# Squares summed by one-column matmuls at the start of a diffusion backbone, and the final features transposed to tokens on partitions before the last norm

## The chip, the cores and the metric

One core of one Trainium2 chip runs the whole program. The time is device microseconds of one execution; runs are compared by their median. A run counts as faster or slower in the chances below when it differs by over 0.2%.

## What is computed

A backbone of two layers over 256 latent and 256 context tokens of width 1024. Each layer is a half-step SwiGLU FFN, a token mixer and another half-step FFN; every sub-layer is preceded by an RMS norm whose gain and shift are modulated by a product of the condition with w_mod. A final RMS norm gives the latent tokens.

```python
def _rmsnorm(h, g):
    y = h32 * lax.rsqrt(jnp.mean(h32 * h32, axis=-1, keepdims=True) + NORM_EPS)
    return (y * g.astype(jnp.float32)).astype(h.dtype)
...
def _ffn_half(h, g, shift, scale, gate, w_in, w_out):
    a, b = jnp.split(_modnorm(h, g, shift, scale) @ w_in, 2, axis=-1)
    return h + 0.5 * gate * ((jax.nn.silu(a) * b) @ w_out)
...
    return _rmsnorm(h, final_norm_g)
```

## The kernel before

The features lie on the partitions: 1024 is eight k-tiles of 128, and a token is a column. hl holds the latent tokens, hc the context tokens. All weights are fp32 in memory and are split into a rounded part hi (ACT, line 124) and a rest lo (DVE, line 125); a product is three matmuls (mm3, lines 136 to 138): the weights' hi by the tokens' hi, hi by the tokens' rest, lo by the tokens' hi. unit() makes such a pair of 2048 columns in two halves, from two loads of 512 KB into seven raw buffers on SP's queue.

The program begins with keep_warm: 22 products of the identity with itself (line 106), while the tokens arrive in eight loads. first() is the start of the first FFN. square() squares two k-tiles at a time on ACT (line 231) and adds them up on DVE (lines 237, 239); rstd_cols() sums over the partitions with one-column matmuls (line 255), and rsqrt() takes the root on DVE with Newton steps (lines 208 to 221). mod_slice(k) gives gain and shift of one k-tile: two loads of wm0, eight matmuls in four column groups (line 155), a copy by ACT (mr, line 160), two matmuls with sel (line 163) and two additions on DVE (line 164). After slice 0 eight more keep-warm products run on its buffer. The root is broadcast over the partitions by four matmuls with the identity (line 271), copied to memory by DVE (line 417), and modnorm() makes ut (DVE, line 285), u's hi (ACT, line 288) and u's rest (DVE, line 289) of each half of the tokens.

lead() then multiplies the first three units of w_in k-tile by k-tile as these become ready: for each of eight k-tiles three units by two halves by three matmuls of 512 columns, 144 in all. swiglu() takes the result: sil (ACT line 305, DVE line 306) and its split g (lines 132, 133). The fourth unit and those after it follow one by one. Beside this DVE computes further modulation pieces (line 176). The instruction order of each engine is fixed when the program is built, by a scheduler that works from the dependences and its own estimates; add_manual_dep adds orders that it must keep.

At the end finish() scales the eight k-tiles by the final gain (ACT, line 831), rstd(0) sums the squares, takes the root and broadcasts it, DVE multiplies four tiles (line 834) and SP sends each off (line 835), with features still on partitions.

Of the kernel before, what the change touches and what calls it, by code (L numbers as in the profile page):

```python
# [11 lines left out]
F32 = mybir.dt.float32  # L12
F32R = mybir.dt.float32r
I32 = mybir.dt.int32
AF = mybir.ActivationFunctionType
# [18 lines left out]
def hybrid_kernel(ctx: ExitStack, tc: tile.TileContext, small, conds, xT, wm0, wm, w_in, w_out,  # L34
# [72 lines left out]

    keep_warm(ident, 22)

# [6 lines left out]

    def unit(src, n=2048, behind=None, at=0):

        hi = hip.tile([P, 2048 + 64], F32R, tag="hi", name=nm("hi"))[:, at:at + 2048]
        lo = lop.tile([P, 2048 + 64], F32R, tag="lo", name=nm("lo"))[:, at:at + 2048]  # L120
        for a in range(0, n, 1024):
            b = min(n, a + 1024)
            raw = load(src[:, a:b])
            A.activation(hi[:, a:b], raw, AF.Copy)  # L124
            i = V.tensor_tensor(lo[:, a:b], raw, hi[:, a:b].bitcast(F32), op=ALU.subtract).ins  # L125
            if behind is not None:
                tc.add_manual_dep(i, behind.name, mybir.DependencyInfo(
                    mybir.DependencyClass.NoSync, mybir.DependencyReason.DATA), reason="order")
        return hi, lo
# [18 lines left out]
    def mod_slice(j):  # L148
# [3 lines left out]
        for kk in range(2):  # L152
            for g in range(4):
                kt = 2 * g + kk
                T.matmul(ps[32 * g:32 * g + 32, :256], c32[:, kt, :], raw[kt // 4][:, kt % 4 * 256:(kt % 4 + 1) * 256],  # L155
                         start=(kk == 0), stop=(kk == 1), tile_position=(0, 32 * g))
        if j == 0:
            keep_warm(raw[1], 8)
        rows = wk.tile([P, 256], F32, tag="ut", name=nm("mr"), bufs=4)
        A.activation(rows, ps[:, :256], AF.Copy)  # L160
        pc = stat()
        for c in range(2):
            T.matmul(pc[:, 2 * c:2 * c + 2], rows[:, c * P:(c + 1) * P], sel, start=True, stop=True)
            V.tensor_tensor(mods[0, c][:, :, j], pc[:, 2 * c:2 * c + 2], bias[:, 0, c, j:j + 1].to_broadcast([P, 2]),
                            op=ALU.add)

    def mod_piece(l, c, n, kp):
# [57 lines left out]

    def square(k, v, n=1):
        sq = wk.tile([P, NT], F32, tag="sil", name=nm("sq"), bufs=3)
        if n == 1:
            A.activation(sq[:, :NL], H(k, v), AF.Square)
        else:  # L230
            A.activation(sq.rearrange("p (k n) -> p k n", k=2),
                         hl[k // 2] if v == 0 else hc[k // 4][:, k % 4:k % 4 + 2, :], AF.Square)
        for i in range(n):
            s = sq[:, i * NL:(i + 1) * NL]
            if k + i == 0:
                sq_sum[v] = wk.tile([P, NL], F32, tag=f"ss{v}", name=nm("ss"), bufs=1)
                V.tensor_copy(sq_sum[v], s)
            else:
                V.tensor_tensor(sq_sum[v], sq_sum[v], s, op=ALU.add)  # L239

# [7 lines left out]
    def rstd_cols(*vs):  # L248
        ps = stat()
        n = 2 * len(vs)  # L250
        for i in range(n):
            v, o = vs[i // 2], i % 2 * P
            parts = [sq_sum[v]] + [sq_last[w] for w in (v,) if w in sq_last]
            for j, t in enumerate(parts):
                T.matmul(ps[:, i:i + 1], t[:, o:o + P], mean_col, start=j == 0, stop=j == len(parts) - 1)  # L255
        ms = wk.tile([P, 4], F32, tag="ms", name=nm("ms"))[:, :n]
        V.tensor_scalar(ms, ps[:, 0:n], EPS, None, op0=ALU.add)
# [3 lines left out]

    def rstd(*vs, meanwhile=None):
        n = 2 * len(vs)
        y = rstd_cols(*vs)
        if meanwhile is not None:
            meanwhile()
        for v in vs:
            normed[v] = newest[0]
        pr = stat()
# [40 lines left out]

    def in_unit(l, i, f, behind=None, at=0):
        return [x.rearrange("p (k s c) -> p k s c", k=KT, s=2) for x in unit(w_in[l, i, f], behind=behind, at=at)]

# [94 lines left out]
    def first(g, u):  # L408
        for c in range(2):
            mod_tile(0, c)  # L410
        gain = cst.tile([P, 2, KT], F32, name="gain0_0")
        units = []
        for v in range(2):
            for k in range(0, KT, 2):
                square(k, v, 2)
        pb = gtile(F32)
        V.tensor_copy(pb, rstd(0, 1, meanwhile=lambda: mod_slice(0)))
        pr = [pb[:, a:b] for a, b in HALVES]

# [18 lines left out]
        for k in range(2):  # L438
            ready(k)
            units.append(in_unit(0, 0, k, normed[0]))  # L440
        units.append(in_unit(0, 0, 2))
# [386 lines left out]
    def finish(v):  # L828
        ts = [gtile(F32).rearrange("p (k n) -> p k n", k=2) for _ in range(4)]
        for k in range(KT):  # L830
            A.activation(ts[k // 2][:, k % 2, :], H(k, 0), AF.Copy, scale=sm[:, S_FG + k:S_FG + k + 1])
        pr = rstd(0)[:, :NL].rearrange("p (k n) -> p k n", k=1).to_broadcast([P, 2, NL])
        for j in range(4):
            V.tensor_tensor(ts[j], ts[j], pr, op=ALU.mult)
            nc.sync.dma_start(out[:, 2 * j:2 * j + 2, :], ts[j])

# [45 lines left out]
def build(arrays):  # L882
# [3 lines left out]
    args = [nc.dram_tensor(f"in_{n}", a.shape, F32, kind="ExternalInput").ap() for n, a in arrays]  # L886
    args.append(nc.dram_tensor("out_x", (P, KT, NL), F32, kind="ExternalOutput").ap())
    with tile.TileContext(nc) as tc:
# [12 lines left out]
```

## Time and profile before

| what | us |
|---|---|
| median of 3 runs | 1679.08 |
| lowest and highest | 1678.54, 1679.54 |
| the profiled execution's own time | 1678.37 |
| its span, first to last instruction | 1676.6 |

The profile is of one execution, 0.71 us below the median; 1.77 us lie around its span. Its views are read as follows: the chain of waits goes back from the last instruction to what released each step; a timeline gives an engine's instructions with the idle time before them and what ended it; windows give busy time and the clock that TensorE was granted (1.00 is 2.4 GHz, 0.50 is 1.2 GHz). Matmul ends are modelled, so starts are the safer numbers.

### The profile page before, as it was taken

Reading aid. Unit: us, or ns where it says so; the run is one execution under the profiler, and the core shown is the slowest. Engines: PE = TensorE matmul, PEld = TensorE weight load, DVE = VectorE, ACT = ScalarE, POOL = GpSimd, SP = SyncE. Lnnn points to the kernel's source line nnn. Section 1 sums busy time; section 2 is a strip of 40 time slices with the busy share of each in tenths; the row PEclk is TensorE's granted clock in tenths of the full one; section 3 lists DMA queues with packets and bytes.
Section 4 is the critical chain, followed back from the end, with each engine's and each line's share of the span. In section 5 each row is a group of like instructions: output and inputs, shape, how many; then the busy total and the mean of one; then the engine's idle time right before and its main releaser. Section 6 shows DMA issues by size and latency. Waiting matters only on the chain.

```text
span 1676.6 us, 23555 instructions
## 1 busy us (share of the span) xinstructions
PE 1655.2 (99%) x9368; PEld 1441.9 (86%) x9368; DVE 1114.6 (66%) x2015; ACT 599.7 (36%) x918; POOL 1.3 (0%) x7
## 2 busy tenths in 40 slices
PE   8999999999999999999999999999999999999997
PEld 6788888889998888888898888888988998899997
DVE  5886677578567845855776546544796767685554
ACT  4431222235433222212342223222574444464443
POOL 0000000000000000000000000000000000000000
PEclk9999999999999999999999999999999999999998
DMA  9675555442215634644435544544334333345651
GB/s 326 238 229 178 176 176 192 141 146 91 67 61 184 202 133 140 200 147 138 139 102 173 178 151 151 189 140 149 108 119 139 121 131 126 133 150 202 194 167 50
DMA packets 73263, 258.74 MB, mean 154 GB/s; under 512 B 8129, under 2 KB 8513, under 8 KB 73153
## 3 DMA queue, kind: packets, MB, share of 16 engines
q1 hardware_dynamic: 73152, 257.24, 45.6%
q8 instruction: 73, 1.20, 0.3%
q14 instruction: 38, 0.30, 0.1%
HBM read 256.16 MB, written 1.05 MB: 153 GB/s over the span
## 4 chain that ended last, share of the span: by engine, by line
PE 95%; DVE 3%; ACT 1%; issue 1%; DMA 0%; SPq 0%; DVEq 0%; ACTq 0%
PE mm L137 31%; PE mm L138 31%; PE mm L136 31%; PE st L155 1%; DVE lo L125 1%; PE st L255 1%; ACT hi L124 0%; DMA big<-in_xT 0%; DVE g L133 0%; PE st L271 0%; DVE g L498 0%; DVE u L289 0%; PE st L106 0%; PE st L731 0%; DVE ss L239 0%
## 5 line engine op out<-in xcount | busy, mean ns | idle before, releaser
L124 ACT ACTIVATE hi<-raw 128x1024 fp32r<-128x1024 f32 x346 | 345.4, 1031 | 653.5 <-PE mm L137 460.6
L137 PE MATMUL mm<-u,hi 128*128 128x512 f32 (+1 forms) x1568 | 554.3, 354 | 0.0
L136 PE MATMUL mm<-u,hi 128*128 128x512 f32 (+1 forms) x1568 | 553.0, 354 | 1.2 <-ACT u L288 1.2
L138 PE MATMUL mm<-u,lo 128*128 128x512 f32 (+1 forms) x1568 | 553.6, 354 | 0.0
L125 DVE TENSOR_TENSOR lo<-raw,hi 128x1024 fp32r<-128x1024 f32 x346 | 406.2, 1195 | 56.8 <-ACT hi L124 52.5
L137 PE MATMUL mm<-g,hi 128*128 128x256 f32 (+1 forms) x1000 | 332.8, 333 | 0.8 <-DVE g L133 0.4
L136 PE MATMUL mm<-g,hi 128*128 128x256 f32 (+1 forms) x1000 | 332.6, 334 | 0.7 <-ACT g L132 0.7
L138 PE MATMUL mm<-g,lo 128*128 128x256 f32 (+1 forms) x1000 | 332.4, 333 | 0.0
L136 PEld LDWEIGHTS mm<-u,hi 128*128 128x128 f32 x1568 | 293.9, 188 | 44.5 <-ACT u L288 2.3
L137 PEld LDWEIGHTS mm<-u,hi 128*128 128x128 f32 x1568 | 294.3, 188 | 42.1 <-DVE u L289 1.0
L138 PEld LDWEIGHTS mm<-u,lo 128*128 128x128 f32 x1568 | 293.9, 188 | 41.8 <-issue 1.2
L176 DVE CUSTOM_DVE_ANT_0 prod<-raw,big,sm 128x1024 bf16<-128x1024 f32 x224 | 275.7, 1282 | 0.0
L306 DVE TENSOR_TENSOR sil<-sil,mm 128x512 f32<-128x512 f32 (+1 forms) x90 | 54.3, 604 | 240.6 <-PE mm L138 231.3
L137 PEld LDWEIGHTS mm<-g,hi 128*128 128x128 f32 x1000 | 187.8, 188 | 20.7 <-DVE g L133 1.6
L136 PEld LDWEIGHTS mm<-g,hi 128*128 128x128 f32 x1000 | 187.4, 188 | 20.2 <-ACT g L132 1.0
L138 PEld LDWEIGHTS mm<-g,lo 128*128 128x128 f32 x1000 | 187.8, 188 | 19.0
L368 DVE SCALAR_TENSOR_TENSOR hl<-mm,gate,hl 128x256 f32<-128x256 f32 x96 | 46.4, 483 | 145.2 <-PE mm L138 145.0
L305 ACT ACTIVATE sil<-mm 128x512 f32<-128x512 f32 (+1 forms) x90 | 47.6, 530 | 204.7 <-PE mm L138 204.7
L133 DVE TENSOR_TENSOR g<-sil,g 128x512 fp32r<-128x512 f32 (+1 forms) x92 | 55.2, 600 | 3.2 <-ACT g L132 3.2
L132 ACT ACTIVATE g<-sil 128x512 fp32r<-128x512 f32 (+1 forms) x92 | 50.3, 547 | 9.0 <-DVE sil L306 9.0
L288 ACT ACTIVATE u<-ut,mod 128x256 fp32r<-128x256 f32 x72 | 33.1, 499 | 42.0 <-DVE ut L285 42.0
L138 PE MATMUL mm<-hi,g 128*128 128x256 f32 (+1 forms) x128 | 43.0, 336 | 0.5 <-DVE g L498 0.4
(174 smaller groups left out, 1208.3 us busy)
## 6 DMA issues: line engine op xcount, KB each, us to landing
raw<-in_w_in SPq DMA_DIRECT2D x176, 512.0 KB, 4.5
raw<-in_wm SPq DMA_DIRECT2D x144, 512.0 KB, 4.8
raw<-in_w_out SPq DMA_DIRECT2D x80, 512.0 KB, 4.3
raw<-in_wvg SPq DMA_DIRECT2D x32, 512.0 KB, 4.3
raw<-in_wqk SPq DMA_DIRECT2D x16, 512.0 KB, 4.6
raw<-in_wro SPq DMA_DIRECT2D x16, 512.0 KB, 4.3
raw<-in_w_out SPq DMA_DIRECT2D x16, 256.0 KB, 2.7
raw<-in_wf SPq DMA_DIRECT2D x8, 512.0 KB, 3.8
```

What stands on the lines that cost most here:

```text
L124: A.activation(hi[:, a:b], raw, AF.Copy)
L125: i = V.tensor_tensor(lo[:, a:b], raw, hi[:, a:b].bitcast(F32), op=ALU.subtract).ins
L132: A.activation(hi, src, AF.Copy)
L133: V.tensor_tensor(lo, src, hi.bitcast(F32), op=ALU.subtract)
L136: T.matmul(ps, l[0], r[0], start=first, stop=False)
L137: T.matmul(ps, l[0], r[1], start=False, stop=False)
L138: T.matmul(ps, l[1], r[0], start=False, stop=last)
L176: V.tensor_tensor_reduce(t, raw, crow[v], 1.0, bias[:, l, c, k:k + 1], ALU.mult, ALU.add, mods[l, c][:, v, k:k + 1])
L288: A.activation(u[k][0][:, a:b], t, AF.Identity, bias=s)
L305: i = A.activation(s[:, :n], pab[0][:, :n], AF.Silu).ins
L306: j = V.tensor_tensor(s[:, :n], s[:, :n], pab[1][:, :n], op=ALU.mult).ins
L368: V.scalar_tensor_tensor(H(d, v), ps[:, x - a:y - a], gate[:, v, d:d + 1], H(d, v), op0=ALU.mult, op1=ALU.add)
```

## The change

The keep-warm products at the start use a tile that DVE fills (14 instead of 22). Each pair of squared k-tiles goes straight to PE: four one-column matmuls (line 426 of the new file) add it to four columns of one PSUM bank, in 32 matmuls; DVE adds nothing. Slice 0 runs after the sums, then the root; three keep-warm products on the last squares replace the eight on slice 0's buffer. The first ut reads the broadcast root in PSUM, and the copy to memory comes later. ACT's copy of slice 0 is ordered ahead of the second halves of the first two units' rounding. At the end every scaled k-tile is transposed by PE (line 862), three quarters of them ahead of the sums; the root then is a number per partition, so that the broadcast falls away, and DVE (line 872) and ACT (line 874) multiply two blocks each, which leave in four transfers, three by SP and one by ACT's queue. The output's layout is tokens by features.

```diff
--- before.py
+++ after.py
@@ -105,7 +105,9 @@
         for _ in range(n):
             T.matmul(ps[:, :P], x[:, :P], x[:, :P], start=True, stop=True)
 
-    keep_warm(ident, 22)
+    warm = gtile(F32)[:, :P]
+    V.memset(warm, 1.0)
+    keep_warm(warm, 14)
 
 
     def load(src):
@@ -114,18 +116,23 @@
         nc.sync.dma_start(t[:, :n], src)
         return t[:, :n]
 
-    def unit(src, n=2048, behind=None, at=0):
+    def order(i, behind):
+        tc.add_manual_dep(i, behind.name, mybir.DependencyInfo(
+            mybir.DependencyClass.NoSync, mybir.DependencyReason.DATA), reason="order")
+
+    def unit(src, n=2048, behind=None, at=0, ahead=None):
 
         hi = hip.tile([P, 2048 + 64], F32R, tag="hi", name=nm("hi"))[:, at:at + 2048]
         lo = lop.tile([P, 2048 + 64], F32R, tag="lo", name=nm("lo"))[:, at:at + 2048]
         for a in range(0, n, 1024):
             b = min(n, a + 1024)
             raw = load(src[:, a:b])
-            A.activation(hi[:, a:b], raw, AF.Copy)
+            i = A.activation(hi[:, a:b], raw, AF.Copy).ins
+            if ahead is not None and a:
+                order(i, ahead)
             i = V.tensor_tensor(lo[:, a:b], raw, hi[:, a:b].bitcast(F32), op=ALU.subtract).ins
             if behind is not None:
-                tc.add_manual_dep(i, behind.name, mybir.DependencyInfo(
-                    mybir.DependencyClass.NoSync, mybir.DependencyReason.DATA), reason="order")
+                order(i, behind)
         return hi, lo
 
     def split(hi, lo, src):
@@ -154,15 +161,14 @@
                 kt = 2 * g + kk
                 T.matmul(ps[32 * g:32 * g + 32, :256], c32[:, kt, :], raw[kt // 4][:, kt % 4 * 256:(kt % 4 + 1) * 256],
                          start=(kk == 0), stop=(kk == 1), tile_position=(0, 32 * g))
-        if j == 0:
-            keep_warm(raw[1], 8)
         rows = wk.tile([P, 256], F32, tag="ut", name=nm("mr"), bufs=4)
-        A.activation(rows, ps[:, :256], AF.Copy)
+        i = A.activation(rows, ps[:, :256], AF.Copy).ins
         pc = stat()
         for c in range(2):
             T.matmul(pc[:, 2 * c:2 * c + 2], rows[:, c * P:(c + 1) * P], sel, start=True, stop=True)
             V.tensor_tensor(mods[0, c][:, :, j], pc[:, 2 * c:2 * c + 2], bias[:, 0, c, j:j + 1].to_broadcast([P, 2]),
                             op=ALU.add)
+        return i
 
     def mod_piece(l, c, n, kp):
 
@@ -223,20 +229,14 @@
 
     sq_sum = {}
 
-    def square(k, v, n=1):
-        sq = wk.tile([P, NT], F32, tag="sil", name=nm("sq"), bufs=3)
-        if n == 1:
-            A.activation(sq[:, :NL], H(k, v), AF.Square)
+    def square(k, v):
+        sq = wk.tile([P, NT], F32, tag="sil", name=nm("sq"), bufs=3)[:, :NL]
+        A.activation(sq, H(k, v), AF.Square)
+        if k == 0:
+            sq_sum[v] = wk.tile([P, NL], F32, tag=f"ss{v}", name=nm("ss"), bufs=1)
+            V.tensor_copy(sq_sum[v], sq)
         else:
-            A.activation(sq.rearrange("p (k n) -> p k n", k=2),
-                         hl[k // 2] if v == 0 else hc[k // 4][:, k % 4:k % 4 + 2, :], AF.Square)
-        for i in range(n):
-            s = sq[:, i * NL:(i + 1) * NL]
-            if k + i == 0:
-                sq_sum[v] = wk.tile([P, NL], F32, tag=f"ss{v}", name=nm("ss"), bufs=1)
-                V.tensor_copy(sq_sum[v], s)
-            else:
-                V.tensor_tensor(sq_sum[v], sq_sum[v], s, op=ALU.add)
+            V.tensor_tensor(sq_sum[v], sq_sum[v], sq, op=ALU.add)
 
     sq_last = {}
 
@@ -253,19 +253,21 @@
             parts = [sq_sum[v]] + [sq_last[w] for w in (v,) if w in sq_last]
             for j, t in enumerate(parts):
                 T.matmul(ps[:, i:i + 1], t[:, o:o + P], mean_col, start=j == 0, stop=j == len(parts) - 1)
+        return root(ps, n)
+
+    def root(ps, n):
         ms = wk.tile([P, 4], F32, tag="ms", name=nm("ms"))[:, :n]
         V.tensor_scalar(ms, ps[:, 0:n], EPS, None, op0=ALU.add)
         y = wk.tile([P, 4], F32, tag="rs", name=nm("rs"))[:, :n]
         rsqrt(y, ms, n)
         return y
 
-    def rstd(*vs, meanwhile=None):
-        n = 2 * len(vs)
-        y = rstd_cols(*vs)
-        if meanwhile is not None:
-            meanwhile()
-        for v in vs:
-            normed[v] = newest[0]
+    def rstd(v):
+        y = rstd_cols(v)
+        normed[v] = newest[0]
+        return along(y, 2)
+
+    def along(y, n):
         pr = stat()
         for i in range(n):
             T.matmul(pr[:, i * P:(i + 1) * P], y[:, i:i + 1].to_broadcast([P, P]), ident,
@@ -308,8 +310,9 @@
             mark[:] = [i, j]
         split(g[f][0][:, a:b], g[f][1][:, a:b], s[:, :n])
 
-    def in_unit(l, i, f, behind=None, at=0):
-        return [x.rearrange("p (k s c) -> p k s c", k=KT, s=2) for x in unit(w_in[l, i, f], behind=behind, at=at)]
+    def in_unit(l, i, f, behind=None, at=0, ahead=None):
+        return [x.rearrange("p (k s c) -> p k s c", k=KT, s=2)
+                for x in unit(w_in[l, i, f], behind=behind, at=at, ahead=ahead)]
 
     def lead(g, u, units, a, b, step=None):
 
@@ -410,12 +413,30 @@
             mod_tile(0, c)
         gain = cst.tile([P, 2, KT], F32, name="gain0_0")
         units = []
+
+        ps = acc()
+
+        def sums(v):
+            for k in range(0, KT, 2):
+                sq = wk.tile([P, NT], F32, tag="sil", name=nm("sq"), bufs=3)
+                A.activation(sq.rearrange("p (k n) -> p k n", k=2),
+                             hl[k // 2] if v == 0 else hc[k // 4][:, k % 4:k % 4 + 2, :], AF.Square)
+                for i in range(4):
+                    c = 2 * v + i % 2
+                    T.matmul(ps[:, c:c + 1], sq[:, i * P:(i + 1) * P], mean_col,
+                             start=v == 0 and k == 0 and i == 0, stop=v == 1 and k == KT - 2 and i == 3)
+            return sq
+
+        sums(0)
+        sq = sums(1)
+        rows = mod_slice(0)
+        y = root(ps, 4)
+        keep_warm(sq, 3)
         for v in range(2):
-            for k in range(0, KT, 2):
-                square(k, v, 2)
+            normed[v] = newest[0]
+        at = along(y, 4)
         pb = gtile(F32)
-        V.tensor_copy(pb, rstd(0, 1, meanwhile=lambda: mod_slice(0)))
-        pr = [pb[:, a:b] for a, b in HALVES]
+        pr = [at[:, a:b] for a, b in HALVES]
 
         def ready(k):
             if k:
@@ -437,7 +458,10 @@
 
         for k in range(2):
             ready(k)
-            units.append(in_unit(0, 0, k, normed[0]))
+            if k == 0:
+                V.tensor_copy(pb, at)
+                pr[:] = [pb[:, a:b] for a, b in HALVES]
+            units.append(in_unit(0, 0, k, normed[0], ahead=rows))
         units.append(in_unit(0, 0, 2))
         lead(g, u, units, 0, NT, step)
         return 3
@@ -826,13 +850,29 @@
 
 
     def finish(v):
-        ts = [gtile(F32).rearrange("p (k n) -> p k n", k=2) for _ in range(4)]
-        for k in range(KT):
-            A.activation(ts[k // 2][:, k % 2, :], H(k, 0), AF.Copy, scale=sm[:, S_FG + k:S_FG + k + 1])
-        pr = rstd(0)[:, :NL].rearrange("p (k n) -> p k n", k=1).to_broadcast([P, 2, NL])
-        for j in range(4):
-            V.tensor_tensor(ts[j], ts[j], pr, op=ALU.mult)
-            nc.sync.dma_start(out[:, 2 * j:2 * j + 2, :], ts[j])
+
+        px = [[acc() for _ in range(2)] for _ in range(2)]
+
+        def turn(j):
+            t = gtile(F32).rearrange("p (k n) -> p k n", k=2)
+            for i in range(2):
+                k = 2 * j + i
+                A.activation(t[:, i, :], H(k, 0), AF.Copy, scale=sm[:, S_FG + k:S_FG + k + 1])
+                for n in range(2):
+                    T.transpose(px[n][k // 4][:, k % 4 * P:(k % 4 + 1) * P], t[:, i, n * P:(n + 1) * P], ident)
+
+        for j in range(3):
+            turn(j)
+        y = rstd_cols(0)
+        turn(3)
+        for n in range(2):
+            for h in range(2):
+                o = gtile(F32)
+                if h == 0:
+                    V.tensor_scalar(o, px[n][h], y[:, n:n + 1], None, op0=ALU.mult)
+                else:
+                    A.activation(o, px[n][h], AF.Copy, scale=y[:, n:n + 1])
+                (nc.scalar if n + h == 2 else nc.sync).dma_start(out[n, :, h * NT:(h + 1) * NT], o)
 
     ffn(1, 1, u6, 8, (0,), finish, first_late)
```

The first place is PE at the start, from the last sums to the first matmuls of slice 1 (mean_col is the column of 1/1024, ident the identity, rs the root, mr the copy of a slice). Before:

```order
L255 MATMUL st_229<-mean_col,ss_196 128x1 x2
L255 MATMUL st_229<-mean_col,ss_213 128x1 x2
L155 MATMUL st_259<-raw_255,g_116 32x256 x2
L155 MATMUL st_259<-raw_257,g_116 32x256 x2
L155 MATMUL st_259<-raw_255,g_116 32x256 x2
L155 MATMUL st_259<-raw_257,g_116 32x256 x2
L106 MATMUL st_268<-raw_257 128x128 x8
L163 MATMUL st_279<-sel,mr_277 128x2
L271 MATMUL st_284<-ident,rs_236 128x128 x2
L163 MATMUL st_279<-sel,mr_277 128x2
L271 MATMUL st_284<-ident,rs_236 128x128 x2
```

With the change, from the last two pairs of squares on (mm_188 is the bank of sums):

```order
L426 MATMUL mm_188<-mean_col,sq_225 128x1 x4
L426 MATMUL mm_188<-mean_col,sq_231 128x1 x4
L162 MATMUL st_241<-raw_237,g_116 32x256 x2
L162 MATMUL st_241<-raw_239,g_116 32x256 x2
L162 MATMUL st_241<-raw_237,g_116 32x256 x2
L162 MATMUL st_241<-raw_239,g_116 32x256 x2
L168 MATMUL st_252<-sel,mr_250 128x2
L106 MATMUL st_278<-sq_231 128x128 x2
L168 MATMUL st_252<-sel,mr_250 128x2
L106 MATMUL st_278<-sq_231 128x128
L273 MATMUL st_282<-ident,rs_259 128x128 x4
L162 MATMUL st_312<-raw_308,g_116 32x256 x2
```

The eight keep-warm products between slice 0 and its selection are three, and stand between the selections; all four broadcasts stand together behind both of them. On DVE the first unit's two lo halves stood ahead of the two additions behind the selections, one before each; now both additions and the gain come first, then one lo half, then the first ut.

The second place is ACT at the fourth unit of w_in, behind the lead: hi are the fourth unit's halves and the first of the fifth, sil and g belong to the lead's three units. Before:

```order
L124 ACTIVATE hi_726<-raw_728 128x1024
L305 ACTIVATE sil_711<-mm_358 128x512
L305 ACTIVATE sil_716<-mm_360 128x512
L124 ACTIVATE hi_726<-raw_732 128x1024
L305 ACTIVATE sil_721<-mm_362 128x512
L132 ACTIVATE g_175<-sil_711 128x512
L124 ACTIVATE hi_803<-raw_805 128x1024
```

With the change:

```order
L130 ACTIVATE hi_725<-raw_727 128x1024
L130 ACTIVATE hi_725<-raw_731 128x1024
L307 ACTIVATE sil_710<-mm_357 128x512
L307 ACTIVATE sil_715<-mm_359 128x512
L307 ACTIVATE sil_720<-mm_361 128x512
L139 ACTIVATE g_169<-sil_710 128x512
L130 ACTIVATE hi_802<-raw_804 128x1024
```

The fourth unit's second half moved ahead of all three sil. On DVE its first lo half stood ahead of the three sil products (line 306) and now follows them and a g; on PE the fourth unit starts with four products by its hi alone, and then come four by the fifth unit's hi.

The third place is PE at the end, behind the last product (px, the mm tiles in the new rows, holds the transposed features). Before:

```order
L137 MATMUL mm_14993<-g_14400,hi_14914 128x256
L138 MATMUL mm_14993<-g_14399,lo_14915 128x256
L255 MATMUL st_15027<-mean_col,ss_14823 128x1
L255 MATMUL st_15027<-mean_col,sq_15013 128x1
L255 MATMUL st_15027<-mean_col,ss_14823 128x1
L255 MATMUL st_15027<-mean_col,sq_15013 128x1
L271 MATMUL st_15053<-ident,rs_15034 128x128 x2
```

With the change, the last four of the first twelve transposes and what follows:

```order
L862 MATMUL mm_15015<-ident,g_15032 128x128
L862 MATMUL mm_15017<-ident,g_15032 128x128
L862 MATMUL mm_15015<-ident,g_15032 128x128
L862 MATMUL mm_15017<-ident,g_15032 128x128
L255 MATMUL st_15039<-mean_col,ss_14822 128x1
L255 MATMUL st_15039<-mean_col,sq_15012 128x1
L255 MATMUL st_15039<-mean_col,ss_14822 128x1
L255 MATMUL st_15039<-mean_col,sq_15012 128x1
L862 MATMUL mm_15015<-ident,g_15065 128x128
L862 MATMUL mm_15017<-ident,g_15065 128x128
```

Twelve transposes stand between the last product and the sums, four behind them, and the broadcast is gone.

## Rows read from the trace of the kernel before

**Rows 1.** The page's busy time and share of the span by engine.

```profile
PE 1655.2 (99%) x9368; PEld 1441.9 (86%) x9368; DVE 1114.6 (66%) x2015; ACT 599.7 (36%) x918; POOL 1.3 (0%) x7
```

**Rows 2.** The chain of waits, 0 to 40 us: start, length (us), what.

```profile
13.35 1.01 PE st L255 x4
14.36 1.86 PE st L155 x16
16.23 3.37 PE st L106 x16
...
21.93 0.49 DVE ut L285
...
23.41 0.73 PE mm L136 x2
```

**Rows 3.** The timeline, 0 to 14: start, length, engine, line, operation, count, [idle before].

```profile
9.98 0.61 PE L255 MATMUL st<-mean_col,ss 128*128 128x1 f32 x4 [1.50 <-DVE ss L239]
...
11.65 0.63 ACT L231 ACTIVATE sq<-big 128x512 f32<-128x512 f32 x1 [1.02 <-DMA big<-in_xT]
```

**Rows 4.** Windows of line 106 alone: length, PE and PEld busy, granted clock, DMA share, GB/s.

```profile
1.00:5.50 4.50, 4.14 (x19) 4.14 (x20) 1.00 0.73 228
5.50:8.50 3.00, 2.98 (x27) 2.78 (x25) 1.00 1.02 298
```

**Rows 5.** Windows of all engines: length, PE, PEld, DVE, ACT, POOL, clock, DMA share, GB/s.

```profile
12.00:13.00 1.00, 0.00 (x0) 0.00 (x0) 0.86 (x3) 0.28 (x1) 0.00 (x0) 0.63 1.05 430
13.00:19.00 6.00, 5.65 (x33) 4.37 (x34) 3.31 (x14) 2.38 (x3) 0.00 (x0) 0.50 1.03 416
...
20.00:24.00 4.00, 2.69 (x29) 1.76 (x28) 3.96 (x8) 2.60 (x5) 0.00 (x0) 1.00 0.88 280
...
56.00:68.00 12.00, 12.00 (x67) 9.52 (x67) 11.75 (x24) 1.90 (x4) 0.00 (x0) 1.00 0.63 222
...
1668.00:1670.00 2.00, 0.92 (x4) 0.92 (x4) 0.92 (x6) 0.00 (x0) 0.00 (x0) 0.50 0.00 0
```

**Rows 6.** The timeline, 13 to 25.

```profile
14.40 0.16 DVE L257 TENSOR_SCALAR ms<-st 128x4 f32<-128x4 f32 x1 [1.11 <-PE st L255]
...
16.38 0.16 DVE L221 SCALAR_TENSOR_TENSOR rs<-rb,ry 128x4 f32<-128x4 f32 x1
...
19.83 1.23 DVE L125 TENSOR_TENSOR lo<-raw,hi 128x1024 fp32r<-128x1024 f32 x1
...
21.18 1.07 PE L155 MATMUL st<-raw,g 128*32 128x256 f32 x16
```

**Rows 7.** What SP's queue waited for, 0 to 60: us in total, times, longest.

```profile
SPq L114 <- PE st L155: 26.4, 8, 5.0
```

**Rows 8.** The timeline, 64 to 78.

```profile
67.40 1.06 ACT L124 ACTIVATE hi<-raw 128x1024 fp32r<-128x1024 f32 x1 [3.34 <-PE mm L137]
...
68.37 1.06 ACT L305 ACTIVATE sil<-mm 128x512 f32<-128x512 f32 x2
...
69.92 0.39 PE L136 MATMUL mm<-u,hi 128*128 128x512 f32 x1
...
70.15 0.39 PE L137 MATMUL mm<-u,hi 128*128 128x512 f32 x1
...
70.74 0.64 ACT L132 ACTIVATE g<-sil 128x512 fp32r<-128x512 f32 x1
```

**Rows 9.** The chain of waits, 1660 to 1677.

```profile
1664.83 0.13 PE mm L138
...
1665.99 0.84 PE st L255 x6
...
1668.87 0.17 DVE rs L221
...
1670.34 0.69 DVE g L834
```

**Rows 10.** The timeline of PE, 1235 to 1242: transposes in the middle of the kernel.

```profile
1240.50 1.09 PE L682 MATMUL mm<-ident,g 128*128 128x128 f32 x8 [0.28 <-DVE big L133]
```

More of the change, by code (lines that the diff above doesn't have):

```diff
@@ L886, in build @@
     args = [nc.dram_tensor(f"in_{n}", a.shape, F32, kind="ExternalInput").ap() for n, a in arrays]
-    args.append(nc.dram_tensor("out_x", (P, KT, NL), F32, kind="ExternalOutput").ap())
+    args.append(nc.dram_tensor("out_x", (2, P, D), F32, kind="ExternalOutput").ap())
     with tile.TileContext(nc) as tc:
@@ L899 @@
     y = r.results[0]["out_x"]
-    return np.ascontiguousarray(y.transpose(2, 1, 0).reshape(1, 256, 1024))
+    return np.ascontiguousarray(y.reshape(1, 256, 1024))
```

## Prediction

> **What bounds the kernel now.** The page's busy shares come first: PE works 1655.2 of 1676.6 us [rows 1], so the kernel is a run of matmuls with about 21 us in which PE does nothing. Where those lie is seen in the chain of waits over the first 40 us [rows 2]: the first matmul of the lead starts only at 23.41. Before it PE stands for the squares' sums and then works slowly, since the granted clock falls to 0.63 in 12-13 and to 0.50 in 13-19 [rows 5] and is back at 1.00 in 20-24; slice 0 takes 1.86 us in the chain at the low level, where slice 1 at full clock takes 1.07 [rows 2, 6]. The other hole is the end: the last matmul ends at 1664.95, and the sums, the root, the broadcast, four multiplications and four transfers run to 1676.6 [rows 9]. The change touches these two ends only, but the scheduler moves other work with it. A measurement of this kernel can tell about 0.2%, 3.4 us, from no change.
>
> **The sums.** An fp32 product shows as two records: eight keep-warm calls are 16 of them [rows 2]. In the old start 19 records fill the time to 5.5 at 0.22 us each, the later ones take 2.98/27 = 0.11 [rows 4]. The new keep-warm starts about as early (a DVE memset in place of POOL's identity) and has 28: 19 to 5.5 and 9 more, to 6.5. Then come 32 one-column products, 64 records. Their price is bounded by L255: six records take 0.84 us with the last one's own 0.25 in it, so 0.118 from start to start [rows 9]; at the low clock four take 1.01, or 0.25 each [rows 2]. At 0.115 the sums need 7.4 us and end at 13.8, a little behind the last squares (11.65 + 0.63, and four products more: 13.2) [rows 3]. Before, the last sum ended at 14.36. DVE's sixteen copies and additions go; they had made PE wait, and now nothing needs DVE before the root.
>
> **From the sums to the first product.** The root takes 16.54 - 14.40 = 2.14 us [rows 6], so it is done at 16.0. Slice 0 runs beside it at full clock, 1.07, and is done at 14.9. The eight keep-warm products that took 3.37 us between slice 0 and its use [rows 2] go, three short ones stay. ACT now copies slice 0's result before it rounds weights; DVE adds the bias once the root is out, 16.1 to 16.8 with the gain, then makes the first lo half, 1.23 [rows 6], to 18.0; the four broadcasts run on PE under it. From the first ut to the first product it was 23.41 - 21.93 = 1.48 [rows 2], now 18.0 + 1.48 = 19.5. The copy of the broadcast is off this path. **The first product comes 3.9 us earlier.**
>
> **How much of that is kept.** Between nothing and all 3.9. The lead's k-tiles 2 to 7 each need a slice of modulation weights, and SP waits 26.4 us in the first 60 for slices' products to give a raw buffer back [rows 7]; towards the end of the lead DVE is busy 11.75 of 12 us, with the products of the next modulation piece [rows 5]. Neither gets shorter. What the loads can gain is the hole in 20-24, 280 GB/s beside 416 in 13-19: 4 x 136/416 = 1.3 us [rows 5]. The new order on PE also puts slices 2 and 3 behind more of the first k-tiles' matmuls, which gives some back. I take 0.8 at the lead's end, nearer the low end for the buffers' sake, and keep 0 and 3.9 for the range.
>
> **The fourth unit.** Here the new order costs. Before, the first product of that unit is at 69.92 and goes on unbroken; its lo half stands ahead of the three sil products on DVE, and on ACT its second hi half stands between the sils. Now DVE has three sil products and a g first, so products that need lo come late, and PE's order goes from four products of this unit to the hi of the fifth. On ACT that hi stands behind two hi halves, three sils and a g. The first hi half waits for PE to give its buffer free, so it moves with the lead: 67.40 - 0.8 = 66.6. Then 2 x 1.06 + 3 x 0.53 + 0.64 + 1.06 = 5.4 us [rows 8], to 72.0. PE has done its four products, 0.23 apart [rows 8], at 69.92 - 0.8 + 0.9 = 70.0 and stands about 2 us; before, it was that far at 70.8. **From here on PE is 1.2 us later**, and with PE busy all the way to the last product (no further place in the order differs by more than line numbers and pairs of rows) that stays.
>
> **The end.** Twelve transposes now stand on PE between the last product and the sums. Eight of that kind take 1.09 us [rows 10], 0.117 from start to start, so 1.4; the wait for the last h and its square up to 1665.99 hides 1.0 of it [rows 9]. Then eight records of sums: 1664.95 + 1.4 + 0.95 = 1667.3 in place of 1666.83, 0.4 later. Without that cover all 1.4 would count. The four transposes after the sums lie under the root. The broadcast goes: root to first multiplication was 1670.34 - 1669.04 = 1.3 [rows 9]. So the first result is ready 0.9 earlier. Four multiplications of up to 0.69 are split between DVE and ACT, where DVE did them in series beside the transfers. If the flow of the transfers sets the end, 0.9 is the gain; if the last issue does, up to 2. I take 0.9, since the first bytes start the same flow.
>
> **Sum.** +1.2 - 0.9 = +0.3 on the profiled execution's 1678.37, 1678.7. That execution lies 0.7 below the median of the runs, 1679.08, so the forecast is **1679.4**: no difference that can be told. Its own range, from a hold at the fourth unit of 1 to 3 us, is 1678.2 to 1680.5.
>
> **Rival: the clock falls during the sums (slower).** No row shows one-column products alone for long. Those at 9.98 [rows 3] are the only PE work between the keep-warm and 13.35, and the clock is 0.63 in 12-13 and 0.50 after [rows 5]; at the end it is 0.50 in 1668-1670, behind sums and the root's pause. Against it: the new stretch has hardly a pause, 0.92 us of work for each 1.0 us of squares, and the keep-warm kept 1.00. Price: half the sums at 0.25 instead of 0.115, 32 x 0.135 = 4.3, slice 0 at the low level 0.8, broadcast 0.4: 5.5 us, the first product at 25.0, 1.6 later than before. The 0.8 that was kept is lost and 1.6 added, 2.4 more than my sum, 1681.8; a clock that comes back only after the first products adds about 0.23 for each of the first few, 1 us or so: 1682.4 in the middle. It decides from a clock at 0.50 in 10 to 16 on. The Trainium skill (TensorE: Matmul & The Clock Gate, section A second HAM failure mode: psum-queue depth-cycling) tells of a kernel whose PE pauses briefly and often between groups of matmuls and so swings between both clock levels; that would be this rival, 1682.4 against 1679.4, and the trace before, with its long pauses, neither bears it out nor excludes it.
>
> **Rival: the fourth unit isn't held.** If the hi of the fifth unit comes in time, PE keeps its 0.8: -0.8 - 0.9 = -1.7, 1677.4. For it: the hold hangs on one row of ACT. Against: each of its parts has a measured length.
>
> **Rival: the early start is kept (faster).** If the lead moves as a whole by 3.9, the hold stays (ACT's first hi half moves with PE, so PE ends 2.0 - 3.9 = 1.9 ahead): -1.9 - 0.9 = -2.8, 1676.3. If nothing is held either, -4.8, 1674.3. Against: SP's waits and the full DVE. That the change doesn't do what it says (sums past 15.4, first product no earlier) needs the low clock, and is in the first rival.
>
> **How the numbers follow.** My forecast 0.52, the clock 0.20, no hold 0.13, early start kept 0.15 (0.06 without a hold). Slower by over 0.2% is past 1682.4: half of the clock's case and 0.03 for other rows that the scheduler moved, 0.13. Faster is below 1675.7: 0.06, and 0.06 from tails of the two faster cases with a larger gain at the end, 0.12. The rest is 0.75. The range 1675.9 to 1682.3 leaves about 0.12 out on either side.
>
> **What the new profile would show.** One-column products without a break from 6.5 to 13.8 with the clock at 1.00 throughout; the root from 13.85 to 16.0; the first product at 19.5, the fourth unit's first at about 69.1, a PE pause of some 2 us behind four of its products, ended by ACT's hi; sums at the end 0.4 later behind the last product, and the first output transfer 0.9 earlier. A granted clock of 0.50 anywhere in 9 to 23 would make the forecast wrong upwards; a lead that ends before 67, or no pause at the fourth unit, downwards.

## The result, and the profile after

The changed kernel takes 1688.21 us (median of 6 runs, 1687.61 to 1692.46) beside 1679.12 before: slower, a ratio of 1.006 with a 95% interval of 1.0049 to 1.0072. Two of the six lie near 1692, at a mean granted clock of 0.990 and 0.991 instead of 0.992 to 0.993. The forecast of 1679.4 and its range missed; what happened is the first rival, the clock, and it cost 8.8 us over the forecast where the rival gave 3.0. The profiled execution took 1687.8 us; its span is 1685.7 us, 9.1 more than before.

The page's busy shares of the changed kernel show that PE is not idle longer; it is busy 11.6 us longer [rows 1], with nearly the same number of instructions:

```profile
PE 1666.8 (99%) x9410; PEld 1450.3 (86%) x9410; DVE 1107.9 (66%) x1998; ACT 600.7 (36%) x920; POOL 1.3 (0%) x7
```

The windows of the changed kernel (length, PE, PEld, DVE, ACT, POOL, granted clock, DMA share, GB/s) show when:

```profile
6.00:9.00 3.00, 3.00 (x27) 3.00 (x26) 0.00 (x0) 1.33 (x3) 0.00 (x0) 1.00 1.01 336
9.00:12.00 3.00, 3.00 (x20) 3.00 (x19) 0.00 (x0) 1.82 (x3) 0.00 (x0) 0.64 0.96 324
...
14.00:16.00 2.00, 2.00 (x11) 2.00 (x11) 0.00 (x0) 0.00 (x0) 0.00 (x0) 0.50 1.03 420
...
22.00:24.00 2.00, 1.85 (x9) 1.59 (x9) 1.51 (x3) 0.28 (x1) 0.00 (x0) 0.50 0.97 371
...
28.00:30.00 2.00, 2.00 (x13) 0.57 (x12) 0.57 (x1) 0.00 (x0) 0.00 (x0) 0.50 0.00 0
30.00:32.00 2.00, 1.75 (x10) 1.42 (x9) 0.19 (x2) 1.33 (x2) 0.00 (x0) 0.92 0.63 209
```

The granted clock is 1.00 to 9, falls in 9-12 and is 0.50, the level of 1.2 GHz, until 30. Before, it was 0.50 from 13 to 19 [rows 5]. The view gives 1.00 from the start on, but the records of the keep-warm products start 0.21 us apart up to 6.4 and 0.11 from there, as they did before up to 5.5 [rows 4]; by their pace the full level lasts here from 6.4 to 9.9 only. PE had no pause ahead of the fall: it is busy 3.00 of 3.00 us in 6-9 and in 9-12. What it ran from 7 on are the sums alone, seen in the windows of their line (length, PE and PEld busy with counts, clock, DMA share, GB/s):

```profile
7.00:9.00 2.00, 2.00 (x19) 2.00 (x19) 1.00 0.99 316
9.00:10.00 1.00, 1.00 (x10) 1.00 (x10) 0.93 0.92 238
10.00:11.00 1.00, 1.00 (x6) 1.00 (x6) 0.50 0.94 324
...
12.00:14.00 2.00, 2.00 (x11) 2.00 (x10) 0.50 1.03 420
```

The counts take in records that a window cuts. The timelines (start, length, what) give the price of a record, 23 in 2.71 us at the full level and 36 in 7.82 us at the low one:

```profile
7.14 2.71 PE L426 MATMUL mm<-mean_col,sq 128*128 128x1 f32 x23
...
10.23 7.82 PE L426 MATMUL mm<-mean_col,sq 128*128 128x1 f32 x36
```

From start to start that is 0.11 us up to 9.8 and 0.21 us after. The chain of waits of the changed kernel (start, length, what) gives the places:

```profile
1.36 5.80 PE st L106 x28
7.16 10.89 PE mm L426 x64
18.05 1.93 PE st L162 x16
...
23.09 2.06 PE st L273 x8
...
26.65 1.22 PE mm L143 x2
...
28.30 1.85 PE st L162 x12
```

The sums end at 18.05, where 13.8 was forecast and 14.36 was the end before. Slice 0 then runs at the low level (1.93), the broadcasts take 2.06, the first product comes at 26.65 and the rest of slice 1 again runs at the low level (1.85). The loads stop too: 0 GB/s in 28-30 above, because SP waits for slices' products to free raw buffers, longer than before [rows 7]:

```profile
SPq L116 <- PE st L162: 29.4, 8, 7.7
```

The fourth unit is held as forecast. In its timeline the first four products run from 78.47, and the next waits 1.14 us for ACT's hi:

```profile
78.47 0.39 PE L143 MATMUL mm<-u,hi 128*128 128x512 f32 x1
...
79.07 0.64 ACT L139 ACTIVATE g<-sil 128x512 fp32r<-128x512 f32 x1
79.17 0.40 PE L144 MATMUL mm<-u,hi 128*128 128x512 f32 x1
79.59 1.06 ACT L130 ACTIVATE hi<-raw 128x1024 fp32r<-128x1024 f32 x1
...
80.71 0.50 PE L143 MATMUL mm<-u,hi 128*128 128x512 f32 x1 [1.14 <-ACT hi L130]
```

The end is shorter, as forecast. The timeline of the changed kernel's end:

```profile
1675.06 0.28 PE L145 MATMUL mm<-g,lo 128*128 128x256 f32 x1
...
1675.18 1.47 PE L862 MATMUL mm<-ident,g 128*128 128x128 f32 x12
...
1677.47 0.16 DVE L260 TENSOR_SCALAR ms<-st 128x2 f32<-128x2 f32 x1 [1.15 <-PE st L255]
...
1679.68 1.41 DVE L872 TENSOR_SCALAR g<-mm,rs 128x512 f32<-128x512 f32 x2
1679.74 1.27 ACT L874 ACTIVATE g<-mm,rs 128x512 f32<-128x512 f32 x2 [3.33 <-DVE rs L227]
1680.45 1.31 SPq L875 DMA_DIRECT2D out_x<-g  x3
```

Before:

```profile
1664.67 0.28 PE L138 MATMUL mm<-g,lo 128*128 128x256 f32 x1
...
1666.85 0.16 DVE L257 TENSOR_SCALAR ms<-st 128x2 f32<-128x2 f32 x1 [0.92 <-PE st L255]
```

From the last product's start to ms it is 2.41 us; before it was 2.18. To the span's end it is 10.6 instead of 11.9.

The starts of some products in the timelines of all kernels, with their times, make one table. "145th" is the fourth unit's first product, the "201st" lies behind the hold; from there to about 1200 us every kernel runs at the same pace, so its column is what the start costs. These columns and the span are of one execution each, which can lie up to 2 us off the median (1676.18 in e8_mix, 1682.86 in e6_dve, 1690.81 in e3_kw22). The ratio is to runs of the kernel before beside each version (medians of 1678.87 to 1679.15).

| kernel | first | 145th | 201st | span | median us | ratio to before (95%) |
|---|---|---|---|---|---|---|
| before | 23.41 | 69.92 | 82.61 | 1676.6 | 1679.12 | |
| changed | 26.65 | 78.47 | 92.98 | 1685.7 | 1688.21 | 1.0060 (1.0049 to 1.0072) |
| e1_end | 24.03 | 70.52 | 83.21 | 1675.9 | 1677.87 | 0.9995 (0.9986 to 1.0004) |
| e2_w64 | 20.64 | 71.15 | 85.61 | 1679.3 | 1681.97 | 1.0017 (1.0008 to 1.0027) |
| e3_kw22 | 26.96 | 80.51 | 94.98 | 1688.6 | 1689.0 | 1.0056 (1.0039 to 1.0072) |
| e4_kw8 | 28.03 | 76.09 | 90.59 | 1683.3 | 1685.48 | 1.0033 (1.0022 to 1.0044) |
| e5_hold | 19.87 | 70.41 | 83.14 | 1676.9 | 1678.02 | 0.9997 (0.9987 to 1.0006) |
| e6_dve | 25.48 | 75.64 | 88.37 | 1681.1 | 1684.81 | 1.0033 (1.0019 to 1.0047) |
| e7_w128 | 20.79 | 69.25 | 82.00 | 1676.6 | 1677.04 | 0.9988 (0.9978 to 0.9997) |
| e8_mix | 21.54 | 68.98 | 81.71 | 1674.4 | 1677.84 | 0.9994 (0.9985 to 1.0003) |
| e9_among | 27.17 | 80.75 | 95.22 | 1689.0 | 1691.35 | 1.0078 (1.0061 to 1.0094) |

The balance of the change: 92.98 - 82.61 = +10.4 at the start, 10.6 - 11.9 = -1.3 at the end, +9.1 in all. In e1_end, which changes nothing there, the profiled start is 0.6 later than before: differences of that size in the first columns say nothing.

### The profile page after: what moved, and what is told of

Read it like the earlier page. It is cut to its first block, busy times and chain, and to the rows that moved or that the text cites. A ratio compares the mean times of both kernels' runs of the same rounds, so it can differ in the third digit from the quotient of the medians.

```text
span 1685.7 us, 23618 instructions
## 1 busy us (share of the span) xinstructions
PE 1666.8 (99%) x9410; PEld 1450.3 (86%) x9410; DVE 1107.9 (66%) x1998; ACT 600.7 (36%) x920; POOL 1.3 (0%) x7
## 4 chain that ended last, share of the span: by engine, by line
PE 96%; DVE 2%; ACT 1%; issue 1%; DVEq 0%; ACTq 0%
PE mm L144 31%; PE mm L143 31%; PE mm L145 31%; PE mm L426 1%; PE st L162 1%; ACT hi L130 1%; DVE lo L133 0%; PE st L255 0%; PE st L106 0%; PE st L273 0%; DVE g L140 0%; DVE ut L287 0%; ACT u L290 0%; DVE g L522 0%; DVE u L291 0%
```

## The experiments

Three theories stood for the 10.4 us: that one-column products do not hold the granted clock (clock), that the clock fell for the shortened keep-warm and the waits between squares (waits), and that the new order delays slices and loads whatever the clock is (order).

### e1_end: the end alone

The kernel before with the new finish() and output, nothing else.

> The kernel before with the end of the change alone (transposes, no broadcast, four blocks on two engines). All theories agree on the place: the sums behind the last product 0.4 us later, the first output transfer about 0.9 to 1.1 us earlier, nothing else moved: 1678.0 us against 1679.1, a ratio of 0.9994. If the end costs something, the time is over 1679.1 and the start of the change costs less than 10 us.

Measured: 1677.87 against 1679.15 beside it, 1.3 us less, within what the runs can tell (the interval takes in 1). The profile shows it at the place: its last product starts at 1665.29 and the span ends at 1675.9, 10.6 us as in the changed kernel, 11.9 before. The end gains, so the start costs more than the whole difference.

### e2_w64: sums 64 columns wide

```diff
-    V.memset(warm, 1.0)
+    V.memset(warm, 1.0 / D)
...
-                    T.matmul(ps[:, c:c + 1], sq[:, i * P:(i + 1) * P], mean_col,
+                    T.matmul(ps[:, c * P:c * P + 64], sq[:, i * P:(i + 1) * P], warm[:, :64],
...
-        y = root(ps, 4)
+        y = root(ps.rearrange("p (c w) -> p c w", w=P)[:, :, 0], 4)
```

The order of every engine's instructions is the same as in the changed kernel. Beside the width, the tile of the keep-warm products holds 1/1024 instead of 1, since the sums now read it in place of the column of 1/1024.

> The changed kernel with each sum made 64 columns wide instead of one (the same 32 products at the same places; the root reads one column of each block). Theory clock (one-column products do not hold the granted clock, and all else follows from that): the clock stays at 1.00 from 6 to 20, the sums end at about 14, the first product of the lead comes at 19.5, the hold at the fourth unit stays at about 2 us, and the time is 1679 (1677 to 1681). Theory waits (the clock falls for the shortened keep-warm and the waits for squares): it falls as before and the time stays at 1688. Theory order (the slices of weights come late because of the new order and the raw buffers, whatever the clock): first product early, but 1684 or more.

The windows of the sums' line in e2_w64:

```profile
7.00:9.00 2.00, 1.84 (x17) 1.71 (x17) 1.00 1.04 306
9.00:10.00 1.00, 1.00 (x11) 1.00 (x11) 1.00 0.89 221
10.00:11.00 1.00, 1.00 (x11) 1.00 (x11) 1.00 0.91 256
...
12.00:14.00 2.00, 1.77 (x16) 1.64 (x15) 1.00 1.02 416
```

The clock is 1.00 throughout and the same 64 records are done at 14.2 instead of 18.05, although each gives 64 times the columns. The first product comes at 20.64 instead of 26.65 and the 201st at 85.61 instead of 92.98: 7.4 of the 10.4 us go with the width of the sums. That shows the clock theory, and waits falls: the keep-warm is as short, and PE even stands for squares here (1.84 of 2.00 us busy in 7-9, 1.77 in 12-14) and keeps 1.00. That the value in the keep-warm tile plays no part was not tested by itself: every version with wide sums holds 1/1024 and every version of the changed kernel that lost the clock holds 1. Against it stands that the keep-warm ends at 7 in the changed kernel, and the clock falls at 9.9, while the sums run on the same numbers in both. The time, 1681.97, lies above the range expected; 3.0 us of loss at the start remain at the full clock and are the share of the order theory (e5_hold and e7_w128, below), and the profiled execution lost about another 1 at 1240 to 1250, where its clock dipped.

### e3_kw22: the longer keep-warm back

```diff
-    keep_warm(warm, 14)
+    keep_warm(warm, 22)
```

> The changed kernel with 22 keep-warm products at the start as before, instead of 14. Theory clock: the sums begin about 1 us later, the clock still falls to 0.50 while they run, some 3 us after the last keep-warm product, and the time is 1687 to 1690. Theory waits: the clock stays at 1.00 and the time is 1679 to 1682.

Measured: 1689.0. The windows of e3_kw22 show the clock falling in 14-16, with PE busy all the time:

```profile
12.00:14.00 2.00, 2.00 (x20) 2.00 (x19) 0.00 (x0) 1.43 (x3) 0.00 (x0) 1.00 1.03 420
14.00:16.00 2.00, 2.00 (x12) 2.00 (x11) 0.00 (x0) 0.46 (x1) 0.00 (x0) 0.54 1.02 418
```

The sums begin 2.2 us later than in the changed kernel (9.21 instead of 7.00) and the clock falls 4.3 later, 5 us behind the last keep-warm product and not the some 3 expected: the start of the sums alone does not set the moment. With the same order behind them the fourth product of the lead comes 0.3 later (30.39). In this execution the clock then fell a second time, during the lead's first products:

```profile
32.00:34.00 2.00, 1.43 (x6) 0.90 (x6) 1.45 (x6) 0.50 (x2) 0.00 (x0) 1.00 0.75 246
34.00:36.00 2.00, 1.53 (x4) 1.21 (x5) 2.00 (x4) 2.00 (x4) 0.00 (x0) 0.66 0.82 293
36.00:38.00 2.00, 2.00 (x6) 1.54 (x6) 2.00 (x3) 1.25 (x2) 0.00 (x0) 0.50 0.86 299
```

From the fourth to the 145th product it is then 50.1 us where the changed kernel has 48.4: the other 1.7 of the 2.0 us by which its 201st product is later. The longer keep-warm moves the first fall and saves nothing, so the shortened keep-warm is not the cause.

### e4_kw8: the eight products behind slice 0 back

```diff
+        if j == 0:
+            keep_warm(raw[1], 8)
         rows = wk.tile([P, 256], F32, tag="ut", name=nm("mr"), bufs=4)
```

> The changed kernel with the eight keep-warm products behind slice 0 put back. Theory clock: the clock falls during the sums as in the changed kernel, which end at 18; the eight products bring it back at about 23 instead of 30, so that the first products, slice 1 and the loads that wait for its buffers come sooner: 1683 to 1686. Theory order: nothing gained, 1688 or more.

Measured: 1685.48, 2.7 less than the changed kernel. Its windows:

```profile
20.00:22.00 2.00, 2.00 (x10) 2.00 (x11) 0.19 (x2) 1.99 (x3) 0.00 (x0) 0.50 0.42 133
22.00:24.00 2.00, 2.00 (x12) 2.00 (x12) 0.12 (x2) 0.28 (x1) 0.00 (x0) 0.56 0.33 129
24.00:26.00 2.00, 1.85 (x16) 1.64 (x15) 1.96 (x5) 0.00 (x0) 0.00 (x0) 1.00 0.55 195
```

With the eight wide products the clock is back at about 24, where the changed kernel has it at 30. The first product is 1.4 later for them and for slice 1, which the scheduler now puts ahead of it as a whole, but the 201st is 2.4 earlier. So the fall's length counts for itself: products that do nothing but keep PE at work cost time ahead of the first product and here gave more back.

### e5_hold: the fourth unit's order

```diff
-        lead(g, u, units, 0, NT, step)
-        return 3
+        return 3, lead(g, u, units, 0, NT, step, lambda: in_unit(0, 0, 3))
...
+            order(j, behind)
```

On the base of e2_w64, lead() calls the unit ahead of its swiglu(), and the sil products of the lead (line 308 of the changed kernel) are ordered behind the unit's first lo half.

> The kernel of e2_w64 with the fourth unit's loads and both its halves emitted ahead of the lead's sil products, and the first sil product ordered behind the fourth unit's first lo half. If the hold at the fourth unit is what the order of ACT and DVE costs there, the matmul four places behind the lead's end follows without a pause as in the kernel before, and the time falls by 1.8 us, from 1682.0 to 1680.2. Rival: the pause only moves on to the fifth unit, whose lo halves now come later on DVE, and the time stays within 0.5 of 1682.

The timeline of e5_hold: the fourth unit runs on without a pause, with its lo in place (line 148) as the fifth product:

```profile
70.41 0.40 PE L146 MATMUL mm<-u,hi 128*128 128x512 f32 x1
...
71.00 2.01 ACT L132 ACTIVATE hi<-raw 128x1024 fp32r<-128x1024 f32 x2
71.10 0.39 PE L147 MATMUL mm<-u,hi 128*128 128x512 f32 x1
...
71.33 0.40 PE L148 MATMUL mm<-u,lo 128*128 128x512 f32 x1
```

From the 145th to the 201st product it is 12.73 us instead of 14.46 in e2_w64: 1.73 less, as expected, and nothing of it comes back later. The time, 1678.02, fell by 4.0, more than the order explains; 0.8 lies ahead of the first product, where nothing was changed, and the rest in the spread of runs (1679.6 to 1684.6 for e2_w64).

### e6_dve: squares summed on DVE again

```diff
-                    T.matmul(ps[:, c:c + 1], sq[:, i * P:(i + 1) * P], mean_col,
-                             start=v == 0 and k == 0 and i == 0, stop=v == 1 and k == KT - 2 and i == 3)
+                        V.tensor_tensor(sq_sum[v], sq_sum[v], s, op=ALU.add)
...
-        y = root(ps, 4)
+        y = rstd_cols(0, 1)
```

> The changed kernel with the squares summed on DVE as before, all else as changed (14 keep-warm products, three in place of eight behind slice 0, the new end). Theory that the one-column sums alone cost the 9 us: 1678 to 1680. Theory that the missing keep-warm work costs its own part: PE stands still between 6.5 and about 13, the clock falls there and no dense work brings it back before the lead's own products, as late as 24 to 30, so the time is 1683 to 1687, though the sums are off PE.

Measured: 1684.81. With the sums undone 5.8 us of loss remain at the 201st product. Its windows show an idle PE and the same low clock, back in 24-26, by the lead's first product (25.48) and not behind it as expected:

```profile
9.00:12.00 3.00, 0.00 (x0) 0.00 (x0) 2.69 (x10) 1.11 (x2) 0.00 (x0) 0.87 0.94 302
12.00:14.00 2.00, 0.65 (x4) 0.22 (x4) 0.85 (x2) 0.63 (x1) 0.00 (x0) 0.50 1.02 418
...
24.00:26.00 2.00, 1.49 (x9) 0.36 (x13) 2.00 (x5) 0.91 (x2) 0.00 (x0) 0.79 0.68 242
```

But the scheduler has put slice 0 ahead of the sums here, which waits for its weights, and the sums stand behind it and its first selection; they come at 17.39 where before they came at 13.35 [rows 2]:

```profile
13.35 3.12 PE L162 MATMUL st<-raw,g 128*32 128x256 f32 x16 [7.17 <-DMA raw<-in_wm]
...
17.39 1.84 PE L255 MATMUL st<-mean_col,ss 128*128 128x1 f32 x8
```

So taking the sums off PE alone does not undo the loss. The keep-warm work that is missing, during which the clock used to come back by 19 [rows 5], is one cause of what remains, with the 2.4 us of e4_kw8; the late sums are another, and the shares were not separated.

### e7_w128 and e8_mix: versions meant to beat both

e7_w128 is e2_w64 with 128 columns. The scheduler answers to the width with another order: half of the weights' rounding ahead of slice 0's copy on ACT, the fourth unit's first lo half ahead of the sil products on DVE.

```diff
-                    T.matmul(ps[:, c * P:c * P + 64], sq[:, i * P:(i + 1) * P], warm[:, :64],
+                    T.matmul(ps[:, c * P:(c + 1) * P], sq[:, i * P:(i + 1) * P], warm,
```

> As e2_w64, with sums 128 columns wide; the scheduler orders ACT and DVE in another way for it: the fourth unit's first lo half stands ahead of the sil products, and half of the weights' rounding ahead of slice 0's copy. Clock at 1.00 from 6 on; sums no longer than with 64 columns (to 14); no hold at the fourth unit: 1679.5 to 1680.5. If wide products cost by their columns, the sums end after 15 and the time is over 1681.

Measured: 1677.04, a ratio of 0.9988 (0.9978 to 0.9997): the only version here whose interval lies below 1, though its 0.12% is less than the 0.2% that counts as faster. It lies 2.5 below the range expected. Its windows:

```profile
9.00:12.00 3.00, 3.00 (x30) 3.00 (x29) 0.00 (x0) 2.21 (x4) 0.00 (x0) 1.00 0.96 340
...
22.00:24.00 2.00, 2.00 (x11) 1.43 (x10) 1.65 (x4) 0.91 (x1) 0.00 (x0) 1.00 1.04 414
...
26.00:28.00 2.00, 2.00 (x10) 1.48 (x10) 2.00 (x4) 1.11 (x2) 0.00 (x0) 1.00 1.03 401
```

No hold, clock at 1.00, loads at 400 GB/s and more up to 28. The first product comes at 20.79 as in e2_w64, the 145th at 69.25 instead of 71.15: the other order, which came with the width, is worth 1.9 us in the lead, and with the hold gone the 201st comes 3.6 earlier.

e8_mix keeps the order of the kernel before (slice 0 beside the root, a copy of the broadcast), with 14 keep-warm products, wide sums, none of the eight products, and the new end.

```diff
-            keep_warm(raw[1], 8)
...
-                square(k, v, 2)
+                    T.matmul(ps[:, c * P:c * P + 128], sq[:, i * P:(i + 1) * P], warm[:, :128],
```

> A version meant to beat both: the order of the kernel before (root, then slice 0 beside it, copy of the broadcast), 14 keep-warm products, sums on PE 128 columns wide, none of the eight keep-warm products, and the new end. If the early start survives to the lead's end, 1676 or less; if slices and their buffers take it back as in e2_w64, 1678 to 1679, the end's 1.1 alone.

Measured: 1677.84, 0.9994 (0.9985 to 1.0003). The first product is 1.9 earlier, the 145th 0.9. The expected 1678 to 1679 was the case in which slices and buffers take most back; it came out a little below.

### e9_among: one wide product among the narrow ones

```diff
+                keep_warm(sq, 1)
             return sq
```

> The changed kernel with its one-column sums as they are, and one 128-column keep-warm product on the same squares behind each group of four sums. If what the clock lacks is wide work on PE, as e2_w64 suggests, some wide work among the narrow may do: the clock at 1.00 throughout, the sums and products (0.92 + 0.23 for each pair of k-tiles) ended at about 16, two later than in e2_w64, the hold still there: 1683 to 1685. If one product in five is too little, the clock falls while they run and the time is 1688 or more. If the width of the sums was not the cause, the same fall as in the changed kernel, from about 10 on.

Measured: 1691.35, the slowest of all. Its windows with PE busy throughout:

```profile
10.00:11.00 1.00, 1.00 (x12) 1.00 (x11) 0.00 (x0) 0.51 (x2) 0.00 (x0) 1.00 0.97 367
11.00:12.00 1.00, 1.00 (x7) 1.00 (x7) 0.00 (x0) 0.28 (x1) 0.00 (x0) 0.52 1.00 406
```

The clock stands at 1.00 to 11 and is 0.52 in 11-12: one wide product in five does not keep it, and the later ones run at the low level themselves. That the fall comes a microsecond later than in the changed kernel is not shown to be their doing. The keep-warm products are the same instructions in both, and their records reach the quick pace at 4.2 here and at 6.4 there: one execution differs from another by more than that. The fourth product of the lead is 0.5 later than in the changed kernel (30.59 instead of 30.09); most of the remaining loss is a second fall, as in e3_kw22 (0.50 in 36-38).

## Why the prediction was wrong

**The likeliest case was chosen wrongly.** The step that failed first stands under the sums: a price of 0.115 per record taken for all 64, with the clock at 1.00, because PE would have hardly a pause. The rows of before could not decide it; the sums at 9.98 and the idle time behind them [rows 3, 5] stood together. I let the absence of pauses decide. PE had none, and the clock fell all the same; in e2_w64 the same products, made wider, kept it. The pauses of which the Trainium skill tells (TensorE: Matmul & The Clock Gate, section A second HAM failure mode: psum-queue depth-cycling) were thus not the mechanism in the changed kernel: the level fell once, without any, and came back once. The second fall of e3_kw22 and e9_among does come behind pauses of PE (1.43 and 1.53 of 2.00 us busy in 32-36 of e3_kw22); the changed kernel has such pauses too and did not fall there, and why is open.

**The rival's price was too small.** It gave 1682.4. Its 4.3 for the sums came near by luck: the sums ended 3.9 later than in e2_w64, but with 37 records at 0.21 instead of half of the 64 at 0.25. The last record's own length stands in that 0.25, which the 0.118 beside it leaves out. Slice 0, with 0.8 in the rival, adds only 0.1: it took 1.93, but in e2_w64 also 1.85, since it waits there for its weights. From the sums' end to the first product it is 8.6 us against 6.5 in e2_w64, so 2.1 more: 0.9 for the broadcasts, given as 0.4, and 1.1 that the rival left out, since ACT's copy, both selections and the fillers stand one behind another ahead of the broadcasts, all at the low level but ACT's. And the low level lasts to 30, through the first products and slice 1: 1.2 more by the fourth product (30.09 against 22.90, 7.2 in all). The 201st product's 7.4 is reached there; nothing later adds to it.

**The early start was taken as a reserve.** The rival set the 5.5 us against the 3.9 of the early start and let the lead lose nothing more. But the lead loses after the first product with the clock up or down: 4.0 us in e2_w64, from 2.8 ahead of the kernel before to 1.2 behind it, and 5.3 in the changed kernel, from 3.2 behind to 8.6. I had put that loss down to SP's waits and a full DVE, that is to a pace which a later start would meet anyway. It is no such floor: the loads wait for the slices' products on PE, so they move with PE (none in 28-30), and e7_w128 loses 2.0 of its early 2.6 where e2_w64 loses 4.0. The forecast of 0.8 kept at the lead's end was wrong by 2.0 even at the full clock (1.2 late in e2_w64). Which of the rows that e7_w128 moved gives these back was not separated.

**The first product** at full clock came at 20.64, 1.1 after the 19.5 of the working: the sums took until 14.2, and the second half of slice 0's weights was waited for.

**The fourth unit** was right: 72.0 - 70.8 = 1.2 with a lead of 0.8, thus 2.0 of hold, against 1.8 measured (10.37 - 8.55), ended by ACT's hi as the order shows, and gone in e5_hold.

**The end** was right in sign and place. The sums come 0.2 later and not 0.4, the first output transfer 1.0 earlier (5.39 us behind the last product's start instead of 6.43) and not 0.9, and the span's end 1.3 earlier.

## What to carry to other kernels

A PE that is busy is not a PE whose clock is up. Work that is moved onto PE to fill a pause should be made wide where width is free: here the same 32 products end 4 us sooner at 64 columns than at one, and the whole start is 7 us shorter. When keep-warm work is cut, find first what else in that stretch holds the clock, and price the whole stretch up to the next dense work at the low level, with the loads that wait on it. And where a scheduler sets the order, compare its rows far behind the edit: 2 us lay in the order of the fourth unit, 50 us after the code that changed.

## What the runs showed of the hardware that was not expected

The granted clock fell from 1.00 to 0.50 while PE ran one-column products back to back (1.00 of 1.00 us busy in 10-11), stayed there through matmuls of 2, 128 and 256 columns with small pauses, and came back at 30, after the lead's first products of 512 columns had run at the low level. In e6_dve it was back by 25, ahead of any product of 512 columns. With one product in five 128 columns wide it fell as well. In e3_kw22 and e9_among it came back at 31 and fell once more, to 0.50 in 36-38. At full clock a record of 64 columns took no longer than one of one column: 11 in 10-11 of e2_w64, 19 in 7-9 of the changed kernel, 0.11 us from start to start in both; with 128 columns there were 30 in 9-12 of e7_w128.
